# A two-pass path for the last five experts of a mixture-of-experts layer, behind one runtime branch

## The chip, the cores and the metric

The kernel runs on one core of a Trainium2 chip. The metric is the device time of one launch, in microseconds (us); beside it stands the span of one profiled execution, from its first to its last instruction. Engines are named as the profile names them: PE is TensorE's matmul, PEld its weight load, DVE is VectorE, ACT is ScalarE, POOL is GpSimd, SP is SyncE, which issues all the DMAs.

## The reference, cut to what matters

A two-layer decoder trunk on 256 tokens of width 2048, in float32. The second layer ends in a top-2-of-8 mixture of SwiGLU experts:

```python
def moe_swiglu(x, w_router, w_gu, w_down):       # x: 256 tokens x 2048
    logits = xt @ w_router                       # 256 x 8
    top_vals, top_idx = lax.top_k(logits, 2)
    gates = ...                                  # softmax over the two, 0 elsewhere
    for e in range(8):
        y = y + gates[:, e:e + 1] * swiglu(xt, w_gu[e], w_down[e])   # 2048 -> 2 x 1408 -> 2048
```

With the reference's own inputs (its default seed) the router gives the eight experts 42, 47, 57, 114, 53, 34, 109 and 56 tokens, as its formulas give when they are evaluated. These counts are data: the program learns them only when it runs.

## The kernel before

Every matmul of a weight runs in three passes, because float32 is kept as a pair of rounded parts. `load` (L98 to L110) issues one DMA from SP into a `raw` buffer (4 x 512 columns on 128 partitions, 1 MB; 768 KB where the block is 384 wide or only three chunks deep). ACT casts it to `wh` (L107), DVE subtracts to get the remainder `wl` (L108). The pools give five `raw` buffers and four of `wh` and of `wl`. `mm3` (L117 to L119) then multiplies, for each 128-row chunk of the weight, x-high by `wh`, x-high by `wl` and x-low by `wh`, with the 128 token slots as the stationary operand and up to 512 weight columns moving.

In `moe` every expert takes at most 128 tokens at once. `top2` picks experts, triangular matmuls turn the picks into positions, and `gather` builds for a pair of experts a 0/1 matrix `Dt` and multiplies it with the tokens (L837), so that PE itself collects the tokens of both experts, transposed, in 64 matmuls of 256 columns; ACT copies the results to `xe` (L839). `slots` inside it transposes `Dt` and picks the gate of each slot. The gather of the first pair runs inside `lead`, between the token casts and the first weight loads. The later pairs are gathered in four quarters during the down projection of the expert before them.

`expert_up` runs six accumulations of 16 chunks (gate and up, 512, 512 and 384 columns wide) and, for each width, `swiglu`: ACT applies silu (L527), DVE multiplies (L528), PE transposes (L181), ACT and DVE split the result (L174, L175). `expert_down` runs four accumulations of 11 chunks; ACT and DVE scale and split each (`yh` L896, `yl` L897), PE spreads it back over the two token tiles (L900, L901), DVE adds it to `h` (L234) and, for the last expert, takes the statistics (L236). One expert is 36 loads: 16 + 8 of `odd_moe_gu`, 8 + 4 of `odd_moe_down`, together 2048 x 2816 x 4 + 1408 x 2048 x 4 bytes = 34.6 MB.

The experts run in the order 0 to 7, written out, so that a scheduler at build time can weave the instructions of neighbouring stages together on each engine; each engine then runs its own list in order. Behind the last expert SP loads the gains and biases of the last LayerNorm (`gb`, L192), `final_norm` writes the output, and a branch (L729) stands ready for an expert with more than 128 tokens. Every engine takes that branch by itself: it loads the value into a register (L728) and compares. Here it is not needed and its body is jumped over.

## Time and profile before

| | |
|---|---|
| time, median of 3 runs (lowest to highest) | 2174.81 us (2173.45 to 2175.77) |
| the profiled execution: its own time | 2175.96 us |
| the profiled execution: span, first to last instruction | 2174.2 us |
| mean granted TensorE clock (1.0 is 2.4 GHz) | 0.994 |
| moved by DMA | 537.80 MB, mean 247 GB/s |

The profiled execution is one run and lies within 0.06% of the median. A busy PE in the profile is not PE at its peak: each matmul is shown until its modelled end, so neighbours overlap; how fast matmuls follow one another is read from their starts. DVE and ACT show an instruction's whole duration too, and the next may start some 0.08 us before the end shown.

### The profile page before, as it was taken

Reading aid. Unit: us, or ns where it says so; the run is one execution under the profiler, and the core shown is the slowest. Engines: PE = TensorE matmul, PEld = TensorE weight load, DVE = VectorE, ACT = ScalarE, POOL = GpSimd, SP = SyncE. Lnnn points to the kernel's source line nnn. Section 1 sums busy time; section 2 is a strip of 40 time slices with the busy share of each in tenths; the row PEclk is TensorE's granted clock in tenths of the full one; section 3 lists DMA queues with packets and bytes.
Section 4 is the critical chain, followed back from the end, with each engine's and each line's share of the span. In section 5 each row is a group of like instructions: output and inputs, shape, how many; then the busy total and the mean of one; then the engine's idle time right before and its main releaser. Section 6 shows DMA issues by size and latency. Waiting matters only on the chain.

```text
span 2174.2 us, 24450 instructions
## 1 busy us (share of the span) xinstructions
PE 2140.0 (98%) x9955; PEld 1781.5 (82%) x9956; DVE 1456.7 (67%) x1225; ACT 1146.6 (53%) x962; POOL 1.6 (0%) x6
## 2 busy tenths in 40 slices
PE   9999999999999999999999999999999999999996
PEld 7888888888888888888788887888888888888884
DVE  5443566554454644556676546898889888888988
ACT  5444355343333433343644335766766767676764
POOL 0000000000000000000000000000000000000000
PEclk9999999999999999999999999999999999999998
DMA  8544645555454554545544643899989999998995
GB/s 347 217 147 145 233 180 208 211 194 191 157 215 172 213 189 169 204 169 218 213 182 166 235 155 117 320 352 357 340 331 367 347 336 342 346 352 322 371 351 213
DMA packets 82198, 537.80 MB, mean 247 GB/s; under 512 B 9504, under 2 KB 10656, under 8 KB 28192
## 3 DMA queue, kind: packets, MB, share of 16 engines
q1 hardware_dynamic: 82080, 536.18, 66.3%
q8 instruction: 80, 1.31, 0.2%
q14 instruction: 38, 0.31, 0.0%
HBM read 534.04 MB, written 2.10 MB: 247 GB/s over the span
## 4 chain that ended last, share of the span: by engine, by line
PE 93%; DVE 3%; ACT 2%; DMA 1%; issue 0%; SPq 0%; DVEq 0%; ACTq 0%
PE acc L118 29%; PE acc L119 28%; PE acc L117 28%; PE ps L181 2%; DVE wl L108 1%; PE ps L837 1%; ACT wh L107 1%; PE ps L900 1%; DMA raw<-in_odd_moe_down_dram 1%; DMA raw<-in_even_w_in_dram 1%; PE ps L901 1%; ACT lnT L259 0%; PE ps L575 0%; PE acc L135 0%; PE acc L629 0%
## 5 line engine op out<-in xcount | busy, mean ns | idle before, releaser
L108 DVE TENSOR_TENSOR wl<-raw,wh 128x2048 fp32r<-128x2048 f32 (+2 forms) x519 | 1121.3, 2178 | 391.5 <-ACT wh L107 390.8
L107 ACT CAST wh<-raw 128x2048 fp32r<-128x2048 f32 (+2 forms) x519 | 935.4, 1824 | 442.1 <-PE acc L119 399.3
L118 PE MATMUL acc<-wl,xh 128*128 128x512 f32 x928 | 363.3, 392 | 1.1 <-DVE wl L108 1.1
L117 PE MATMUL acc<-wh,xh 128*128 128x512 f32 x928 | 361.8, 390 | 0.1
L119 PE MATMUL acc<-wh,xl 128*128 128x512 f32 x928 | 361.6, 390 | 0.0
L118 PE MATMUL acc<-wl,xe 128*128 128x512 f32 (+1 forms) x752 | 280.7, 373 | 0.1
L119 PE MATMUL acc<-wh,xe 128*128 128x512 f32 (+1 forms) x752 | 279.4, 372 | 0.0
L117 PE MATMUL acc<-wh,xe 128*128 128x512 f32 (+1 forms) x752 | 278.6, 371 | 0.5 <-ACT wh L107 0.5
L118 PE MATMUL acc<-wl,hTh 128*128 128x512 f32 x704 | 277.3, 394 | 1.1 <-DVE wl L108 1.0
L119 PE MATMUL acc<-wh,hTl 128*128 128x512 f32 x704 | 276.1, 392 | 0.0
L117 PE MATMUL acc<-wh,hTh 128*128 128x512 f32 x704 | 274.8, 391 | 0.0
L118 PEld LDWEIGHTS acc<-wl,xh 128*128 128x128 f32 x928 | 174.4, 188 | 37.0 <-DVE wl L108 1.5
L117 PEld LDWEIGHTS acc<-wh,xh 128*128 128x128 f32 x928 | 174.2, 188 | 37.1 <-ACT xh L174 0.5
L119 PEld LDWEIGHTS acc<-wh,xl 128*128 128x128 f32 x928 | 174.4, 188 | 35.7 <-DVE xl L175 0.2
L118 PEld LDWEIGHTS acc<-wl,xe 128*128 128x128 f32 x752 | 141.2, 188 | 21.2 <-DVE wl L108 1.8
L117 PEld LDWEIGHTS acc<-wh,xe 128*128 128x128 f32 x752 | 141.2, 188 | 20.7 <-ACT wh L107 0.8
L118 PEld LDWEIGHTS acc<-wl,hTh 128*128 128x128 f32 x704 | 132.3, 188 | 30.3 <-DVE wl L108 3.5
L119 PEld LDWEIGHTS acc<-wh,xe 128*128 128x128 f32 x752 | 141.3, 188 | 19.0
L117 PEld LDWEIGHTS acc<-wh,hTh 128*128 128x128 f32 x704 | 132.3, 188 | 28.3
L119 PEld LDWEIGHTS acc<-wh,hTl 128*128 128x128 f32 x704 | 132.4, 188 | 26.4
L174 ACT CAST hTh<-ps 128x512 fp32r<-128x512 f32 (+1 forms) x46 | 26.2, 569 | 180.4 <-PE ps L181 180.4
L117 PE MATMUL acc<-wh,x0h 128*128 128x512 f32 x256 | 104.1, 409 | 2.5 <-ACT wh L107 2.5
(201 smaller groups left out, 1820.0 us busy)
## 6 DMA issues: line engine op xcount, KB each, us to landing
raw<-in_odd_moe_gu_dram SPq DMA_DIRECT2D x128, 1024.0 KB, 6.9
raw<-in_even_ffn_gu_dram SPq DMA_DIRECT2D x88, 1024.0 KB, 4.8
raw<-in_odd_moe_down_dram SPq DMA_DIRECT2D x64, 1024.0 KB, 7.0
raw<-in_odd_moe_gu_dram SPq DMA_DIRECT2D x64, 768.0 KB, 6.1
raw<-in_even_ffn_down_dram SPq DMA_DIRECT2D x44, 1024.0 KB, 4.8
raw<-in_odd_w_in_dram SPq DMA_DIRECT2D x32, 1024.0 KB, 4.8
raw<-in_even_w_in_dram SPq DMA_DIRECT2D x30, 1024.0 KB, 5.0
raw<-in_odd_moe_down_dram SPq DMA_DIRECT2D x32, 768.0 KB, 6.8
```

What stands on the lines that cost most here:

```text
L107: nc.scalar.copy(wh, raw)
L108: self.wl_ins = nc.vector.tensor_tensor(wl, raw, wh.bitcast(F32), ALU.subtract)
L117: mm(acc, xh, wh, start=first, stop=False)
L118: mm(acc, xh, wl, start=False, stop=False)
L119: mm(acc, xl, wh, start=False, stop=last)
L174: self.nc.scalar.copy(hi, src)
L181: self.nc.tensor.transpose(ps[:, j * P:(j + 1) * P], src[:, j * P:(j + 1) * P], self.ident)
L837: mm(o, xtok[t, c // 8][part][:, cs], Dt[t].rearrange("p a b -> p (a b)"), start=j == 0 and t == 0, stop=t == 1, skip_group_check=True)
L900: nc.tensor.matmul(ps, DT[:, t, :], yh, start=True, stop=False)
L901: nc.tensor.matmul(ps, DT[:, t, :], yl, start=False, stop=True)
```

## The change

Expert 0 runs as before, but its tokens are gathered alone. While it runs, a new step `order` on DVE sorts experts 1 to 7: those with more than 64 tokens first, the rest behind, in their old order. It leaves the permuted expert numbers (`ids`), positions and gates, and the count of experts above 64 (`full`). SP loads `ids` into registers, and the weight DMAs of all later experts take their address from them. The first two of the sorted list run in the old three-pass path. Then all engines meet one `If`: if at most two experts are above 64, the other five run as `slim_expert`; if not, the `Else` runs the old path for them.

A slim expert has 64 slots. Its stationary operand holds x-high in columns 0 to 63 and x-low in columns 64 to 127, so a chunk needs two matmuls (with `wh` and with `wl`) and the rows 64 to 127 of the accumulator hold the low part's product. `fold` copies the accumulator by ACT and adds its lower rows to its upper ones with one more matmul; this is done for the six up accumulations. The down projection does the same with the split `hT`, and the spreading over the tokens, whose slot matrix names the 64 slots in both halves, sums the two. Nothing of the body is issued ahead of the branch (`EARLY = 0`), and the pools keep their sizes. The pieces of `expert_down` become the functions `down_loads` and `scatter`, the pieces of `gather` the function `slots`, with the same instructions.

```diff
+SLIM = 64
+EARLY = 0
+FATS = 2
+REST = NEXP - 1
...
-        nc.sync.dma_start(raw, src)
+        self.issued = nc.sync.dma_start(raw, src)
...
+        self.fold = pm.tile([P, P], F32R, tag="fold", name="fold", bufs=1)
+        nc.gpsimd.memset(self.fold[:, SLIM:].bitcast(F32), 0.0)
+        nc.gpsimd.tensor_copy(self.fold[:, :SLIM], self.ident[:, SLIM:])
...
-        gat = self.gather(xtok, [pos1[t][:, 0:2] for t in range(NT)], gg, 0, 0)
+        gat = self.gather(xtok, [pos1[t][:, 0:1] for t in range(NT)], gg, 0, 0, num=1)
...
+        def gate_cols(t, gates, at, num):
+            gv = gg[t][:, 1, at:at + 2 * num].rearrange("p (e s) -> p e s", s=2)
+            nc.scalar.copy(gv[:, :, 0], gates)
+            nc.vector.tensor_tensor(gv[:, :, 1], gates, gv[:, :, 0].bitcast(F32), ALU.subtract)
...
-        for e in range(NEXP):
-            cur = gat
-            hT = self.expert_up(e, cur, e % 2, None if e else first)
-            if e == 0:
+        many = pm.tile([P, REST], F32, tag="many", name="many", bufs=1)
+        nc.vector.tensor_scalar(many, cnt[:, 1:NEXP], float(SLIM), None, ALU.is_gt)
+        ids, posP, full = [], [], pm.tile([P, 1], I32, tag="full", name="full", bufs=1)
+
+        def gather(k, num):
+            return self.gather(xtok, [posP[t][:, k:k + num] for t in range(NT)], gg, NEXP + k, 0, num=num)
+
+        def gather_slim(k, num):
+            return self.gather_slim(xtok, [posP[t][:, k:k + num] for t in range(NT)], num)
+
+        def prepare():
+            order = self.order(many, pos1, gates, gate_cols, posP, full)
+            ins, v = nc.values_load_multi_w_load_instructions(
+                order[0:1, :], engines=[mybir.EngineType.SP], min_val=1, max_val=REST)
+            self.after(ins[0], self.issued)
+            ids.extend(v)
+
+        hT = self.expert_up(0, gat, 0, first, prepare)
+        gat[4]()
+        cur, gat = gat, gather(0, FATS)
+        gat[4]()
+        self.expert_down(0, cur, 0, hT, True, None, gat[3])
+        for p in range(FATS):
+            hT = self.expert_up(ids[p], gat, p)
+            self.expert_down(ids[p], gat, p, hT, False, None)
+        full_v = nc.values_load(full[0:1, 0:1], min_val=0, max_val=REST)
+        src = i["odd_moe_gu"][ids[FATS], 0]
+        early = [self.load(src[k]) for k in range(EARLY)]
+        with tc.If(full_v < FATS + 1) as slim:
+            at = 0
+            A, step = gather_slim(FATS, 2)
+            for q in range(4):
+                step(q)
+            for k in range(FATS, REST):
+                ahead = partial(gather_slim, k + 1, REST - k - 1) if k == FATS + 1 else None
+                nxt = self.slim_expert(ids[k], k - FATS - at, A, gg, NEXP + k, fstats if k == REST - 1 else None,
+                                       early if k == FATS else None, ahead)
+                if nxt is not None:
+                    A, at = nxt, 2
+        with slim.Else():
+            for k in range(FATS, REST, 2):
+                num = min(2, REST - k)
+                gat = gather(k, num)
                 gat[4]()
-            step = None
-            if e % 2 and e + 1 < NEXP:
-                gat = self.gather(xtok, [pos1[t][:, e + 1:e + 3] for t in range(NT)], gg, e + 1, 0)
-                gat[4]()
-                step = gat[3]
-            self.expert_down(e, cur, e % 2, hT, e == 0, fstats if e == NEXP - 1 else None, step)
+                for q in range(4):
+                    gat[3](q)
+                for p in range(num):
+                    hT = self.expert_up(ids[k + p], gat, p, early=None if k + p > FATS else early)
+                    self.expert_down(ids[k + p], gat, p, hT, False, fstats if k + p == REST - 1 else None)

         G, B = self.load_gb(i["odd_ln2_g"], i["odd_ln2_b"])
         self.final_norm(fstats, G, B)
...
+    def order(self, hv, pos1, gates, gate_cols, posP, full):
...
+        self.after(v.tensor_reduce(H, hv, AX.X, ALU.add), self.wl_ins)
+        v.tensor_copy(full, H)
+        v.tensor_tensor(sq, rows(hv), square(C_LOWER), ALU.mult)
+        v.tensor_reduce(rank, sq, AX.X, ALU.add)
+        v.scalar_tensor_tensor(a, e7, H, rank, ALU.add, ALU.subtract)
+        v.tensor_tensor(b, rank, a, ALU.subtract)
+        v.tensor_tensor(b, b, hv, ALU.mult)
+        v.tensor_tensor(a, a, b, ALU.add)
+        v.tensor_tensor(perm, rows(a), square(C_PLACE), ALU.is_equal)
+        v.tensor_scalar(b, e7, 1.0, None, ALU.add)
+        v.tensor_tensor(sq, perm, rows(b), ALU.mult)
+        v.tensor_reduce(b, sq, AX.X, ALU.add)
+        v.tensor_copy(ids, b)
+        for t in range(NT):
+            g = tile("gateP", [P, R], bufs=2)
+            x = tile("posP", [P, R], bufs=2)
+            for dst, src in ((x, pos1[t]), (g, gates[t])):
+                v.tensor_tensor(sq, perm, rows(src[:, 1:NEXP]), ALU.mult)
+                v.tensor_reduce(dst, sq, AX.X, ALU.add)
+            gate_cols(t, g, 2 * NEXP, R)
+            posP.append(x)
+        return ids
+
+    def gather_slim(self, xtok, pos, num):
...
+        slots = self.iota1[:, :SLIM].unsqueeze(1).to_broadcast([P, 2, SLIM])
+        d4 = []
+        for t in range(NT):
+            d = pm.tile([P, num, 2, SLIM], F32R, tag="Dt", name="d4", bufs=2)
+            for p in range(num):
+                nc.vector.tensor_scalar(d[:, p], slots, pos[t][:, p:p + 1], None, ALU.is_equal)
+            d4.append(d)
...
+        def quarter(q):
+            for c in range(4 * q, 4 * q + 4, per):
+                if c % hold == 0:
+                    units[0] = self.unit("xs", shape=[P, hold, num, 2, SLIM])
+                ps = self.ps()
+                for j in range(per):
+                    cs = slice((c + j) % 8 * P, ((c + j) % 8 + 1) * P)
+                    for part in range(2):
+                        o = ps[:, (2 * j + part) * w:(2 * j + part + 1) * w]
+                        for t in range(NT):
+                            mm(o, xtok[t, (c + j) // 8][part][:, cs], d4[t][:, :, 0, :],
+                               start=j == 0 and part == 0 and t == 0, stop=t == 1, skip_group_check=True)
+                for j in range(per):
+                    u = units[0][:, (c + j) % hold]
+                    nc.scalar.copy(u, ps[:, 2 * j * w:2 * (j + 1) * w].rearrange("p (a e s) -> p e a s", a=2, e=num))
+                    A[c + j] = u
+        return (A, d4), quarter
+
+    def slim_expert(self, e, p, gat, gg, col, stats, early, ahead):
...
+        def two(groups, lhs, w):
+            acc = self.acc()
+            n, k0 = sum(g[2] for g in groups), 0
+            for wh, wl, kc in groups:
+                for j in range(kc):
+                    mm(acc[:, :w], lhs(k0 + j), wh[:, j, :], start=k0 + j == 0, stop=False)
+                    mm(acc[:, :w], lhs(k0 + j), wl[:, j, :], start=False, stop=k0 + j == n - 1)
+                k0 += kc
+            return acc
+
+        def fold(acc, w):
+            c = self.pln.tile([P, CB], F32R, tag="lnT", name="low")
+            nc.scalar.copy(c[:, :w], acc[:, :w])
+            mm(acc[:, :w], self.fold, c[:, :w], start=False, stop=True, skip_group_check=True)
+
+        hT = []
+        for b, w in enumerate(EXP_W):
+            accs = [two(self.up_loads(e, b, u, early),
+                        lambda k: A[k][:, p], w) for u in range(2)]
+            for acc in accs:
+                fold(acc, w)
+            nch = w // P
+            s = self.pln.tile([P, CB], F32, tag="lnT", name="silu")
+            nc.scalar.activation(s[:, :w], accs[0][:, :w], AF.Silu)
+            nc.vector.tensor_tensor(s[:, :w], s[:, :w], accs[1][:, :w], ALU.mult)
+            pv = self.transpose4(s, nch)[:, :w].rearrange("p (c t) -> p c t", c=nch)[:, :, :SLIM]
+            h = pm.tile([P, 4, 2, SLIM], F32R, tag="hTh", name="hT2", bufs=3)
+            nc.scalar.copy(h[:, :nch, 0, :], pv)
+            nc.vector.tensor_tensor(h[:, :nch, 1, :], pv, h[:, :nch, 0, :].bitcast(F32), ALU.subtract)
+            hT.append(h)
+        DT, gs = self.slots([d4[t][:, p] for t in range(NT)], gg, col)
+        nxt, step = (None, None) if ahead is None else ahead()
+        for n in range(NCB):
+            if step is not None:
+                step(n)
+            acc = two(self.down_loads(e, n), lambda k: hT[k // 4][:, k % 4], CB)
+            self.scatter(acc, DT, gs, n, False, stats)
+        return nxt
...
+            if then is not None and b == 0:
+                then()
```

## Rows read from the trace of the kernel before

**Rows 1.** The page: busy us (share of the span) xinstructions of each engine.
```profile
PE 2140.0 (98%) x9955; PEld 1781.5 (82%) x9956; DVE 1456.7 (67%) x1225; ACT 1146.6 (53%) x962; POOL 1.6 (0%) x6
```

**Rows 2.** Windows, experts 2 and 5, then five: busy us (x), clock, DMA share, GB/s.
```profile
1538.94:1639.53 100.59, 100.59 (x484) 86.10 (x485) 86.16 (x59) 71.36 (x54) 0.00 (x0) 1.00 0.91 339
...
1840.60:1939.74 99.14, 99.12 (x480) 84.63 (x479) 85.17 (x57) 71.57 (x58) 0.00 (x0) 1.00 0.95 356
...
sum 501.40, PE 500.48 PEld 427.38 DVE 428.36 ACT 357.68 POOL 0.00; mean PE 100.10 PEld 85.47 DVE 85.67 ACT 71.54 POOL 0.00
```

**Rows 3.** Waits from 1538 to 2040 us: us in total, times, longest us.
```profile
ACT wh L107 <- PE acc L119: 28.7, 36, 1.3
...
PEld acc L118 <- DVE wl L108: 3.0, 6, 0.8
```

**Rows 4.** Timeline of PE, start us, us: matmuls of 512 columns.
```profile
1640.23 0.39 PE L118 MATMUL acc<-wl,hTh 128*128 128x512 f32 x1
1640.45 0.39 PE L119 MATMUL acc<-wh,hTl 128*128 128x512 f32 x1
```

**Rows 5.** Timeline of PE: matmuls of 384 columns.
```profile
1705.38 0.33 PE L117 MATMUL acc<-wh,xe 128*128 128x384 f32 x1
1705.55 0.33 PE L118 MATMUL acc<-wl,xe 128*128 128x384 f32 x1
```

**Rows 6.** Timeline of PE: eight gather matmuls of 256 columns.
```profile
1360.34 1.10 PE L837 MATMUL ps<-Dt,xtl 128*128 128x256 f32 x8
```

**Rows 7.** Groups of two experts, 1639.5 to 1840.5 us: busy us, mean ns, idle before.
```profile
L108 DVE TENSOR_TENSOR wl<-raw,wh 128x2048 fp32r<-128x2048 f32 x49 | 110.8, 2288 | 18.1 <-ACT wh L107 18.0
...
L839 ACT CAST xe<-ps 128x512 fp32r<-128x512 f32 x16 | 8.7, 592 | 3.8 <-PE ps L837 3.8
...
L175 DVE TENSOR_TENSOR hTl<-ps,hTh 128x512 fp32r<-128x512 f32 x4 | 2.8, 688 | 0.9 <-ACT hTh L174 0.8
```

**Rows 8.** Windows with the fastest DMA, columns as in rows 2.
```profile
17.50:47.50 30.00, 29.79 (x131) 24.36 (x131) 15.61 (x10) 15.26 (x13) 0.00 (x0) 1.00 1.02 416
...
2017.50:2047.50 30.00, 30.00 (x141) 25.47 (x141) 28.68 (x21) 21.75 (x15) 0.00 (x0) 1.00 0.99 398
2015.00:2065.00 50.00, 50.00 (x233) 42.40 (x232) 47.11 (x33) 36.97 (x25) 0.00 (x0) 1.00 0.99 377
```

**Rows 9.** The buffer raw, 1538.94 to 2040.34 us: time from issue to landing.
```profile
DMA to landing us min/median/max: 4.0/6.7/8.9
```

**Rows 10.** Timeline of ACT in expert 0, with idle time and what ended it.
```profile
1376.46 1.92 ACT L107 CAST wh<-raw 128x2048 fp32r<-128x2048 f32 x1 [0.80 <-PE acc L119]
```

**Rows 11.** Timeline of ACT at the end of expert 2.
```profile
1654.54 0.69 ACT L896 ACTIVATE yh<-acc,gs 128x512 fp32r<-128x512 f32 x1 [2.76 <-PE acc L119]
```

**Rows 12.** Groups of DVE in the router, 1336 to 1347 us.
```profile
L819 DVE TENSOR_SCALAR Dt<-c,pos 128x128 fp32r<-128x128 f32 x4 | 0.9, 284 | 0.0
...
L682 DVE SCALAR_TENSOR_TENSOR pos<-ps,sel 128x8 f32<-128x8 f32 x2 | 0.3, 162 | 0.0
```

**Rows 13.** The branch L729: duration ns min/median/max, first and last start.
```profile
L729 PEldq COMPARE_BRANCH  x1: 3370/3370/3370, 2155.0 to 2155.0; - x1
...
L729 DVEq COMPARE_BRANCH  x1: 72/72/72, 2169.0 to 2169.0; - x1
```

**Rows 14.** Timeline of the kernel's end.
```profile
2152.68 0.69 ACT L896 ACTIVATE yh<-acc,gs 128x512 fp32r<-128x512 f32 x1 [7.84 <-PE acc L119]
...
2157.49 0.74 DVE L224 SCALAR_TENSOR_TENSOR o<-h,mv,gb 128x512 f32<-128x512 f32 x1
```

**Rows 15.** Timeline of SP around the last weight load.
```profile
2134.99 0.33 SPq L106 DMA_DIRECT2D raw<-in_odd_moe_down_dram  x1
...
2136.31 1.23 SPq L192 DMA_DIRECT2D gb<-in_odd_ln_b_dram  x2
```

**Rows 16.** The buffer gb, 2130 to 2174 us: time from issue to landing.
```profile
DMA to landing us min/median/max: 6.2/7.4/8.3
```

**Rows 17.** Windows of the router, columns as in rows 2.
```profile
1340.00:1350.00 10.00, 6.88 (x41) 5.84 (x40) 8.46 (x40) 5.88 (x13) 0.00 (x0) 0.76 0.00 1
```

More of the change, by code (lines that the diff above doesn't have):

```diff
@@ L845, in slots @@
             for p in range(num):
[L846 to L854 removed]
+                DT, gs = self.slots([Dt[t][:, p, :] for t in range(NT)], gg, e + p)
                 DTs.append(DT)
@@ L857, in gather, with slots @@
         return xe, DTs, gss, quarter, slots
-    def expert_up(self, e, gat, p, first=None):
-        i, pm = self.i, self.pm
+    def slots(self, d, gg, col):
+        nc, pm = self.nc, self.pm
+        ps = self.ps()
+        for t in range(NT):
+            nc.tensor.matmul(ps[:, t * 256:(t + 1) * 256], d[t], gg[t], start=t == 0, stop=True,
+                             skip_group_check=True)
+        DT = pm.tile([P, NT, P], F32R, tag="DT", name="DT", bufs=3)
+        pv = ps.rearrange("p (a b) -> p a b", a=2)
+        nc.scalar.copy(DT, pv[:, :, 0:P])
+        gs = pm.tile([P, 1], F32, tag="gs", name="gs", bufs=4)
+        nc.vector.tensor_reduce(gs, pv[:, :, P + 2 * col:P + 2 * col + 2], AX.XY, ALU.add)
+        return DT, gs
@@ new lines, in order, with tile, rows, square @@
+    def order(self, hv, pos1, gates, gate_cols, posP, full):
+        nc, pm = self.nc, self.pm
+        v = nc.vector
+        R = REST
+        def tile(tag, shape, dt=F32, bufs=1):
+            return pm.tile(shape, dt, tag=tag, name=tag, bufs=bufs)
+        def rows(x):
+            return x.unsqueeze(1).to_broadcast([P, R, R])
+        def square(c):
+            return self.c[:, c:c + R * R].rearrange("p (a b) -> p a b", a=R)
+        e7 = self.c[:, C_IOTA7:C_IOTA7 + R]
+        rank, a, b = (tile(f"ord{k}", [P, R]) for k in range(3))
+        H = tile("ordH", [P, 1])
+        ids = tile("ids", [P, R], I32)
+        sq, perm = tile("ordsq", [P, R, R]), tile("perm", [P, R, R])
+        self.after(v.tensor_reduce(H, hv, AX.X, ALU.add), self.wl_ins)
[20 more added lines that the diff above has]
+        return ids
@@ L861, in expert_up @@
+    def expert_up(self, e, gat, p, first=None, then=None, early=None):
+        pm = self.pm
         xe = gat[0]
@@ L873, in expert_up @@
                     continue
-                groups = self.loads(i["odd_moe_gu"][e, b * 2 + u] if b < 2 else i["odd_moe_gu2"][e, u], w)
-                accs.append(self.block(groups, lhs, 0, w))
+                accs.append(self.block(self.up_loads(e, b, u, early), lhs, 0, w))
             hT.append(self.swiglu(pm, accs[0], accs[1], w, w // P, "m"))
+            if then is not None and b == 0:
+                then()
         return hT
@@ L887, in expert_down, with up_loads, down_loads, scatter @@
                 step(n)
-            groups = []
-            for k in range(0, EXP_KC, PIECE):
-                o, kc = k * CB * P, min(PIECE, EXP_KC - k)
-                src = i["odd_moe_down"][e, n][o:o + kc * CB * P].rearrange("(p m) -> p m", p=P)
-                groups.append(self.load(src))
-            acc = self.block(groups, lhs, 0)
-            yh = pm.tile([P, CB], F32R, tag="yh", name="yh", bufs=1)
-            yl = pm.tile([P, CB], F32R, tag="yl", name="yl", bufs=1)
-            nc.scalar.mul(yh, acc, gs)
-            nc.vector.scalar_tensor_tensor(yl, acc, gs, yh.bitcast(F32), ALU.mult, ALU.subtract)
-            for t in range(NT):
-                ps = self.ps()
-                nc.tensor.matmul(ps, DT[:, t, :], yh, start=True, stop=False)
-                nc.tensor.matmul(ps, DT[:, t, :], yl, start=False, stop=True)
-                self.add_stats(t, n, ps, None if stats is None else stats[t], first)
+            acc = self.block(self.down_loads(e, n), lhs, 0)
+            self.scatter(acc, DT, gs, n, first, stats)
+    def up_loads(self, e, b, u, early):
+        i = self.i
+        src = i["odd_moe_gu"][e, b * 2 + u] if b < 2 else i["odd_moe_gu2"][e, u]
+        if early is None or b or u:
+            return self.loads(src, EXP_W[b])
+        return early + [self.load(src[k]) for k in range(EARLY, src.shape[0])]
+    def down_loads(self, e, n):
+        groups = []
+        for k in range(0, EXP_KC, PIECE):
+            o, kc = k * CB * P, min(PIECE, EXP_KC - k)
+            src = self.i["odd_moe_down"][e, n][o:o + kc * CB * P].rearrange("(p m) -> p m", p=P)
+            groups.append(self.load(src))
+        return groups
+    def scatter(self, acc, DT, gs, n, first, stats):
+        nc, pm = self.nc, self.pm
+        yh = pm.tile([P, CB], F32R, tag="yh", name="yh", bufs=1)
+        yl = pm.tile([P, CB], F32R, tag="yl", name="yl", bufs=1)
+        nc.scalar.mul(yh, acc, gs)
+        nc.vector.scalar_tensor_tensor(yl, acc, gs, yh.bitcast(F32), ALU.mult, ALU.subtract)
+        for t in range(NT):
+            ps = self.ps()
+            nc.tensor.matmul(ps, DT[:, t, :], yh, start=True, stop=False)
+            nc.tensor.matmul(ps, DT[:, t, :], yl, start=False, stop=True)
+            self.add_stats(t, n, ps, None if stats is None else stats[t], first)
     def load_consts(self):
```

33 lines of the change are left out of this document (20 added, 13 removed).

## The prediction

> **What bounds the kernel now.** Three views, in this order. The page first: PE is busy 98% of the span [rows 1], but that says nothing of the stage that changes. So the windows next, one for each expert from its first load to the next one's [rows 2]: an expert lasts 100.3 us (501.40 / 5), of which PE is busy 100.10, DVE 85.67, ACT 71.54. The reader is to see that the runner-up is only 15% behind. Last the waits of the same stretch [rows 3]: ACT, whose casts start every weight's way, waits 36 times (28.7 us) for PE to give a buffer back, PE only 3.0 us for DVE. PE sets the pace here, and what a lighter PE is worth depends on what ends last behind it.
>
> **What the two passes take from PE.** Matmuls of 512 columns follow one another every 0.227 us (single steps of 0.22 to 0.23, [rows 4]), of 384 every 0.173 [rows 5], of 256 every (1.10 - 0.28) / 7 = 0.117 [rows 6]. An expert has 64 + 44 chunks of 512 columns and 32 of 384. Three passes are 3 x (108 x 0.227 + 32 x 0.173) = 90.2 us, two are 60.1. To these come six folds (1.3 us), the spreading (16 x 0.23 = 3.7), transposes and slots (1.4) and the gather. Gather matmuls of 128 and 192 columns have no row: half of 0.117 is the lower bound for 128, 0.117 the upper. The three rows lie on a line of 0.055 per 128 columns, so I take 0.06 and 0.09: 64 of each for five experts, 1.9 us for one. PE falls to 68.4 us for an expert. Were nothing else in the way, 5 x 31.7 = 158 us would go.
>
> **What is late next.** DVE. The stage keeps all 36 subtractions; it saves half the width of three `hTl` (0.69 us each whole, [rows 7]), some 0.9 us. Its floor is 85.67 - 0.9 = 84.7 us for an expert. DMA: 34.6 MB at the best rate that held for 30 us, 416 GB/s [rows 8], is 83.2 us. ACT: 71.54, less the pair gather's copies (8.7 for two experts, [rows 7]), plus 2.5 for the slim ones, plus six fold copies of some 0.59 (bounded by the `xe` copy, the same shape out of PSUM): 73 us. Two floors lie within 2 us of each other, fed through small buffers, on engines that run their lists in order, so the pitch p of a slim expert will be above 84.7. I take the share that DVE reached where it was busiest over 30 us, 28.68 / 30 = 0.956 [rows 8]: p = 84.7 / 0.956 = 88.6. The other end: 377 GB/s, the best 50 us [rows 8], gives 91.8; the best whole expert, 356 GB/s [rows 2], gives 97.2.
>
> The Trainium skill, page "DMA: Bandwidth & Descriptors", section Specifications, gives one core a limit of about 358 GB/s from HBM. By that figure p would be an estimated 96.6 and the time 2168.6. The 30 us at 416 GB/s disagree with it, and the measurement decides.
>
> The ring of five `raw` buffers must turn at that pace: 6.7 us from issue to landing at the median [rows 9], 1.92 for the cast [rows 10], 2.29 for the subtraction [rows 7], 10.9 in all, against 5 x 88.6 / 36 = 12.3. It fits with 1.4 us to spare, no more.
>
> **The terms around the stage**, counted from the start of `yh` of expert 2's last block, at 1654.54 [rows 11]; in the new kernel that is the end of the second fat expert.
> (a) The first gather is for one expert: 64 x (0.117 - 0.06) = 3.6 us less PE work in a stretch where PE is busy 9 tenths. Between 0 and -3.6; I take -3.
> (b) `order` is 24 small DVE instructions in one chain, 0.16 to 0.28 us each [rows 12], 4 to 7 us, and twice waits for an ACT copy that can stand behind a cast (2 x 1.92). Queued behind it are the subtractions of expert 0's second width, and PE waits for those. The cover: at 1376.46 ACT already waits for PE to free a `wh` [rows 10], so four loads of 2.8 us (100.3 / 36), 11 us of PE work, are ready. SP's register load of `ids` waits for the chain too, with the rest of expert 0's loads behind it; the same 11 us and the filled `raw` buffers cover it. Between 0 and 5; I take 1, the cover being the larger.
> (c) Entry. No instruction of the body may stand ahead of the branch. ACT's first cast comes behind `yh`: 0.69 + 1.92 us, so the first subtraction can't start before 2.6; DVE also has `yl`, two adds and four compares of 0.28 [rows 12] to do, and eight gather copies of 0.59 compete with the casts. SP runs ahead, passes the branch early and has the five buffers filled. The compare itself cost DVE 0.07 us [rows 13]. Between 2.6 and 8; I take 4. PE stands idle here, but it is not the bound behind it.
> (d) Five slim experts: 5 x 88.6 = 443, and 2 for the last one's statistics, which lay under PE before.
> (e) From the last subtraction to `yh`: three chunks by two passes, 1.6 us.
> (f) Leaving the body, each engine jumps over five unused experts. The one far jump that before shows, PE's, took 3.37 us; DVE's short one 0.07 [rows 13]. DVE's list of five experts holds more than 250 instructions, which is nearer to PE's case: 3.4 us on DVE, ahead of the last norm. Between 0 and 3.4.
> (g) From `yh` to the end as before: 2174.2 - 2152.68 = 21.5 us [rows 14]. The `gb` loads no longer run behind the last weight load [rows 15] but behind SP's jump: last issue + 0.4 + 3.4 + 2 + 8.3 (the longest landing, [rows 16]) = 14. They are needed at last issue + 6.7 + 1.5 + 1.8 + 1.6, then 4.8 (2157.49 - 2152.68) and 3.4 = 19.8. Hidden, with 6 us to spare; if SP must also see its last load land, 1 us late.
> The refactored pieces issue the same instructions and cost nothing; `fold`'s preparation is two POOL instructions, and POOL is idle. PE waits in each fold for ACT, with the next chunks queued behind: PE has 88.6 - 68.4 = 20 us to spare for an expert, and without that cover six folds of about 1 us would count.
>
> Sum: 1654.5 - 3 + 1 + 4 + 443 + 2 + 1.6 + 3.4 + 21.5 = 2128.0 against the span of 2174.2, a gain of 46.2 us. The profiled run took 2175.96, 1.15 above the median; on the median's scale the time is 2174.81 - 46.2 = 2128.6. In general it is 1685.6 + 5 p, and the gain is gone at p = 97.8.
>
> **Rivals.**
> 1. The ring or the DMA sets p. For it: 1.4 us of slack, and landings of up to 8.9 us [rows 9]. Against it: the 416 GB/s. p of 92 to 97, at 94.5 the time is 2158.
> 2. Slower: the ends of the blocks are laid bare. Behind the last subtraction of an up width come 1.8 us of matmuls, the fold copy 0.6, the fold 0.5, silu 0.6, transposes and `hT` 1.0, some 4.5 us that DVE doesn't fill if its list holds the multiply next; behind each down block 2.5 (matmuls and `yh`). 84.7 + 3 x 4.5 + 4 x 2.5 = 108, time 2226. It decides once more than 56% of these 23.5 us are uncovered (p above 97.8). For it: the fold is a new link, and `low` and `silu` share two buffers. Against it: in before the next casts are woven in between.
> 3. Slower: TensorE's clock. Before shows it at 0.76 of full where PE was busy 6.88 of 10 us in short pieces [rows 17]. At the lower level, 1.2 GHz, a slim expert takes 2 x 68.4 = 137 us, time 2370; it decides below a mean granted clock of 68.4 / 97.8 = 0.70. Against it: PE at half speed would have no idle time left, and busy stretches here stand at 1.00.
> The Trainium skill, page "TensorE: Matmul & The Clock Gate", section Part 1, describes this case: a thin matmul stage that waits for its weights falls back to the low clock again and again. By that rule this change would lose; the windows at 398 and 416 GB/s, where data was as fast as here, show 1.00 and disagree.
> 4. The change doesn't do what it says: the `Else` runs. With the counts of the reference's inputs (114 and 109, then 57, 56, 53, 47, 34 in some order) at most two are above 64, so it should not. Then the time is before's plus about 4 for the entry, 3.4 for the exit and 1 for the order: 2183.
> 5. Better: p of 84.7 to 86 and a cheap jump: 2103 to 2115.
>
> **How the numbers follow.** Forecast (p of 86 to 92, 2115 to 2146): 0.55. Rival 1, 0.17. Rival 5, 0.10. Rival 2, 0.10. Rival 3, 0.02. Rival 4, 0.03. No change at all, by a mixture of p near 97.8, 0.03. The lowest sum is p = 84.7 with -3.6, 0, 2.6 and no jump: 2109.1 - 0.6 - 1 - 1.4 - 3.4 = 2103. Upwards rival 1 counts to p = 96, 2166. From 2103 to 2166 holds 0.80; the forecast's own range is 2115 to 2146. Within 0.2% (4.3 us, about what a measurement of this kernel can tell from no change) lie p of 97 to 98.7: 0.05 with the edge of rival 1. Slower: 0.10 + 0.02 + 0.03 - 0.02 for what of them stays near = 0.13. Faster: 0.82.
>
> **What would show it.** In the body's windows: PE's matmul steps still 0.227 but with waits for `wl`; DVE busy some 95%, DMA near 390 GB/s, granted clock 1.00; 443 us between the body's first and last subtraction. DVE's wait at the exit near 3.4 us, and a DMA pause nowhere. I am wrong if DVE is below 90% there (rival 1 or 2: which of them tells who waits, ACT for DMA, or ACT and DVE for PE), if the clock is low, or if matmuls of L117 to L119 keep their number.

## The result, and the profile after

The time is 2186.16 us (median of 5 runs, 2185.47 to 2189.09) against 2174.88 (2173.45 to 2175.77): the ratio is 1.0055, with a 95% interval of 1.004 to 1.007. The change makes the kernel slower by 0.5%; 2128.6 was forecast, in a range of 2103 to 2166. The profiled execution has a span of 2184.4 us, 10.2 more than before.

The slim arm ran. The page shows PE with less to do [rows 1] and DVE the same:

```profile
PE 2055.4 (94%) x9286; PEld 1662.3 (76%) x9286; DVE 1456.7 (67%) x1249; ACT 1148.1 (53%) x994; POOL 1.9 (0%) x8
```

Windows of the second and third slim expert and of the whole body, from its first subtraction to its last (columns as in rows 2):

```profile
1751.65:1851.26 99.61, 81.30 (x336) 60.41 (x337) 84.63 (x61) 70.87 (x61) 0.00 (x0) 0.95 0.94 351
1851.26:1945.81 94.55, 81.55 (x360) 61.02 (x358) 85.03 (x57) 74.12 (x63) 0.00 (x0) 1.00 0.96 364
...
1664.40:2156.70 492.30, 402.41 (x1664) 297.41 (x1664) 424.56 (x284) 352.88 (x291) 0.00 (x0) 0.96 0.93 346
```

An expert takes 98.5 us (492.3 / 5), of which DVE is busy 84.9, and no engine is near 100% any more. DVE idles 13.5 us in each: it is busy 86% of the body, and the prediction's own sign of being wrong was less than 90%. Who makes it wait is told by the waits from 1640 to 2165 us, to be held against [rows 3]:

```profile
ACT low L1018 <- PE acc L1012: 69.6, 27, 4.3
...
DVE wl L119 <- ACT wh L118: 61.7, 47, 6.0
ACT yh L1098 <- PE acc L1012: 42.8, 16, 9.3
...
ACT wh L118 <- DMA raw<-in_odd_moe_gu_dram: 10.5, 14, 1.6
```

Landings are not what is missing (10.5 us). ACT waits 112 us for accumulators (9.3 of them behind the body), and DVE 62 us for casts (6.0 of them ahead of it). The two belong together, as ACT's and then DVE's timeline at the end of an up block show (a block is one accumulation):

```profile
1962.73 1.91 ACT L118 CAST wh<-raw 128x2048 fp32r<-128x2048 f32 x1 [0.64 <-DMA raw<-in_odd_moe_gu_dram]
1965.53 1.91 ACT L118 CAST wh<-raw 128x2048 fp32r<-128x2048 f32 x1 [0.89 <-DMA raw<-in_odd_moe_gu_dram]
1969.49 0.58 ACT L1018 CAST low<-acc 128x512 fp32r<-128x512 f32 x1 [2.05 <-PE acc L1012]
1969.98 5.50 ACT L118 CAST wh<-raw 128x2048 fp32r<-128x2048 f32 x3
```

```profile
1963.03 6.73 DVE L119 TENSOR_TENSOR wl<-raw,wh 128x2048 fp32r<-128x2048 f32 x3
1971.91 8.90 DVE L119 TENSOR_TENSOR wl<-raw,wh 128x2048 fp32r<-128x2048 f32 x4 [2.15 <-ACT wh L118]
```

The cast at 1962.73 is the block's last, the one at 1965.53 the next block's first. Behind that one stands `low` in ACT's list; it needs the old block's last matmuls (PE starts the last at 1969.07), and the other casts of the next block stand behind it. So DVE makes the two last subtractions of the old block and the one of the next for which it has a cast (until 1969.76), and then finds nothing to do until ACT has got `low` out of the way and made one more cast. This is how most ends of blocks stand in the new list: one or two casts of the next block ahead of `low` and of `yh`. The third expert has four, three and two ahead of its first three `low`, and from its first subtraction to the next expert's it takes 94.4 us, where the first, second and fourth take 97.9 to 99.8.

The entry is the second place. ACT, DVE, and a window of 10 us with its granted clock:

```profile
1654.25 0.69 ACT L1098 ACTIVATE yh<-acc,gs 128x512 fp32r<-128x512 f32 x1 [6.57 <-PE acc L130]
1660.22 0.65 ACT L995 CAST xs<-ps 128x256 fp32r<-128x256 f32 x2 [5.29 <-PE ps L991]
...
1662.46 1.91 ACT L118 CAST wh<-raw 128x2048 fp32r<-128x2048 f32 x1
```

```profile
1664.41 2.29 DVE L119 TENSOR_TENSOR wl<-raw,wh 128x2048 fp32r<-128x2048 f32 x1 [6.03 <-ACT wh L118]
```

```profile
1664.00:1674.00 10.00, 10.00 (x44) 9.61 (x44) 7.82 (x4) 9.15 (x16) 0.00 (x0) 0.50 0.56 198
```

From this `yh` to the first subtraction of the body are 10.2 us: ACT's first cast stands behind four copies of the gather (two pairs), and the gather runs at half the clock. The terms of the prediction's sum against this span:

| term | forecast | measured |
|---|---|---|
| up to `yh` of the second fat expert, (a) and (b) | 1652.5 | 1654.25 |
| (c) `yh` to first subtraction | 4 | 10.2 |
| (d) first to last subtraction | 445 | 492.2 |
| (e) last subtraction to `yh` | 1.6 | 3.3 |
| (f), (g) `yh` to the end | 24.9 | 24.5 |
| sum | 2128.0 | 2184.4 |

### The profile page after: what moved, and what is told of

It reads as the page before. It is cut to its first block, busy times and chain, and to the rows that moved or that the text cites. A ratio compares the mean times of both kernels' runs of the same rounds, so it can differ in the third digit from the quotient of the medians.

```text
span 2184.4 us, 23740 instructions
## 1 busy us (share of the span) xinstructions
PE 2055.4 (94%) x9286; PEld 1662.3 (76%) x9286; DVE 1456.7 (67%) x1249; ACT 1148.1 (53%) x994; POOL 1.9 (0%) x8
## 5 line engine op out<-in xcount | busy, mean ns | idle before, releaser
L1012 PE MATMUL acc<-wl,xs 128*128 128x512 f32 (+1 forms) x480 | 192.2, 402 | 42.9 <-DVE wl L119 41.9
L130 PE MATMUL acc<-wh,hTl 128*128 128x512 f32 x484 | 190.3, 393 | 0.0
L129 PE MATMUL acc<-wl,hTh 128*128 128x512 f32 x484 | 189.6, 392 | 0.0
L128 PE MATMUL acc<-wh,hTh 128*128 128x512 f32 x484 | 189.2, 391 | 0.0
L1011 PE MATMUL acc<-wh,xs 128*128 128x512 f32 (+1 forms) x480 | 185.0, 387 | 0.3 <-ACT wh L118 0.3
L1012 PEld LDWEIGHTS acc<-wl,xs 128*128 128x128 f32 x480 | 93.3, 194 | 82.6 <-DVE wl L119 69.7
L1012 PE MATMUL acc<-wl,hT 128*128 128x512 f32 x220 | 92.1, 419 | 26.7 <-DVE wl L119 26.6
L1011 PEld LDWEIGHTS acc<-wh,xs 128*128 128x128 f32 x480 | 93.5, 195 | 14.2 <-ACT wh L118 0.7
L129 PE MATMUL acc<-wl,x0h 128*128 128x512 f32 x256 | 100.6, 394 | 1.4 <-DVE wl L119 1.4
L130 PE MATMUL acc<-wh,xe 128*128 128x512 f32 (+1 forms) x272 | 101.1, 372 | 0.0
```

Of the source, the lines that this page charges most:

```text
L128: mm(acc, xh, wh, start=first, stop=False)
L129: mm(acc, xh, wl, start=False, stop=False)
L130: mm(acc, xl, wh, start=False, stop=last)
L1011: mm(acc[:, :w], lhs(k0 + j), wh[:, j, :], start=k0 + j == 0, stop=False)
L1012: mm(acc[:, :w], lhs(k0 + j), wl[:, j, :], start=False, stop=k0 + j == n - 1)
```

## The experiments

All are edits of the changed kernel. "Body" is the stretch from the first to the last subtraction of the five experts in the profiled execution; "entry" runs from `yh` of the second fat expert to the first subtraction (negative: it starts before that `yh`). The ratio is to runs of the kernel before, taken beside it. The profiled execution is one of a kernel's runs: in run 2 the longest of four (2148.47 to 2156.14 us), in run 14 the shortest (2144.85 to 2153.57), so bodies compare to some us only.

| run | time, us | ratio to before (95%) | entry | body |
|---|---|---|---|---|
| the change | 2186.16 | 1.0055 (1.004 to 1.007) | 10.2 | 492.2 |
| 1 one cast ahead | 2161.98 | 0.9945 (0.9932 to 0.9959) | 10.2 | 469.5 |
| 2 two casts ahead | 2152.75 | 0.9891 (0.9876 to 0.9906) | 9.7 | 463.4 |
| 3 frame alone | 2214.64 | 1.0184 (1.0171 to 1.0198) | 19.6 | 511.0 |
| 4 no branch | 2172.14 | 0.9989 (0.9978 to 0.9999) | -3.2 | 495.2 |
| 5 two ahead, no branch | 2149.87 | 0.9874 (0.9858 to 0.9891) | -3.2 | 470.7 |
| 6 four raw buffers | 2219.46 | 1.0191 (1.0178 to 1.0205) | 9.3 | 519.7 |
| 7 filler in the body | 2188.17 | 1.0062 (1.0048 to 1.0075) | 8.6 | 493.5 |
| 8 two ahead, three early loads | 2914.04 | 1.3399 (1.3381 to 1.3418) | -3.2 | 1231.5 |
| 9 two ahead, casts first | 2154.88 | 0.9900 (0.9885 to 0.9915) | 4.1 | 469.0 |
| 10 two ahead, six raw, three wl | 2157.99 | 0.9920 (0.9906 to 0.9933) | 9.8 | 440.1 |
| 11 9 and 10 together | 2158.78 | 0.9928 (0.9915 to 0.9942) | 4.1 | 447.2 |
| 12 two early loads | 2243.29 | 1.0311 (1.0297 to 1.0325) | -3.2 | 562.1 |
| 13 9 with PE kept busy at the entry | 2144.84 | 0.9859 (0.9842 to 0.9875) | 4.2 | 457.0 |
| 14 2 with PE kept busy at the entry | 2149.30 | 0.9889 (0.9872 to 0.9905) | 4.2 | 458.3 |

**1 and 2: the order of ACT's and DVE's lists.** In the body the loads of the next block are issued in the program before the end of the present one, and the order of some instructions is fixed (`AHEAD` is 1 or 2):

```diff
+            fold(accs[0], w, self.cast_ins)  # first low behind the width's last cast
+            cast, sub = self.peek(AHEAD)     # makes the next block's first loads
+            fold(accs[1], w, cast)           # second low behind that cast on ACT
...
+            self.after(nc.vector.tensor_tensor(s[:, :w], s[:, :w], accs[1][:, :w], ALU.mult), sub)
...
-        nc.scalar.mul(yh, acc, gs)
+        self.after(nc.scalar.mul(yh, acc, gs), cast)
```

> The slim body as in the change, but the cast of the next block's first load stands ahead of the block's last copy (low, yh) in ACT's list, and its subtraction ahead of the block's last product in DVE's list. Theory A (ACT works its list in order, waits 3.5 us at each block's end for the accumulator with the next cast behind, and DVE then waits for that cast): ACT's wait no longer holds back a subtraction; of DVE's 13 us of idle time in a slim expert 6 to 10 go, the pitch of a slim expert falls from 98 to 88 to 92, and the time from 2186 to 2136 to 2156. Theory B (the five raw buffers or the DMA set the pitch): the same bytes and buffers, so the pitch stays at 97 to 99 and the time at 2180 to 2192. Theory C (PE is the bound at its lower clock, 0.92 to 1.00 of full being granted in the slim windows): the time moves by less than 10 us, and PE waits for DVE less only where the clock falls further.

> As the kernel with one cast ahead, but two casts (and their subtractions) of the next block stand ahead of the block's last copy. Theory A: a block's end leaves DVE with 2 x 2.3 us of subtractions instead of one, which covers the whole chain of the last chunk's matmuls, low, fold and silu (4.5 us by the prediction); pitch 86 to 89, time 2125 to 2141, below the one with one cast. Theory B: no further change. Against both: low and yh come later by 1.9 us, and a PSUM buffer is free later; if that counts, it is no better than one ahead, 2136 to 2156.

Theory A holds in direction, and its size was too large: 24 us with one cast and 33 with two, at the same buffers and bytes, both short of their ranges. The names of the runs tell less than the edit does. One cast already stood ahead of every `low` in the changed kernel; what run 1 moves is the first `low` of each width, behind all four casts of the next block instead of mostly one or two, and DVE's multiply, behind the next block's first subtraction. Run 2 puts two casts ahead of the second `low` and of `yh`, where mostly one stood. ACT's and DVE's order were not changed one without the other. The waits from 1700 to 2090 us say which end of block each of the two mended. In run 1:

```profile
ACT wh L119 <- DMA raw<-in_odd_moe_gu_dram: 26.2, 29, 2.4
ACT yh L1129 <- PE acc L1043: 26.1, 12, 3.5
...
ACT low L1049 <- PE acc L1043: 10.0, 10, 1.8
```

In run 2:

```profile
DVE wl L120 <- ACT wh L119: 28.8, 34, 3.2
...
ACT yh L1129 <- PE acc L1043: 6.1, 9, 2.0
```

In the changed kernel the same stretch holds 54.7 us for `low`, 26.1 for `yh` and 42.7 of DVE's waits. In the down blocks one cast stood ahead of `yh` already, so the first edit leaves that wait as it was and the second removes it. What grows is ACT's wait for landings (10.5 to 26.2): the next limit. The pitch, a fifth of the body, stops at 92.7, not at the 86 to 89 expected of two casts.

**3: the frame alone.**

```diff
-        with tc.If(full_v < FATS + 1) as slim:
+        with tc.If(full_v < 1) as slim:
```

> The condition is made false for these inputs, so the five experts take the three-pass path of the kernel before behind the same branch, in the same order of experts. What remains of the change is its frame: the order of the experts, the entry, gathers that no longer lie in an expert's down blocks, and the exit. The prediction put these at 1 + 4 + 3.4 us: 2183. Theory A with the entry as the changed kernel shows it (10.2 us, of which some 3 lie at any expert's end, exit 4.3): 2184 to 2190, so that the slim stage itself gains next to nothing over three passes. A rival: gathers bare at the head of each pair cost PE's own time no more than before, but ACT and DVE wait: up to 2196.

Both were too low. This timeline of ACT at its entry shows why it is no measure of the slim stage's frame:

```profile
1662.33 0.74 ACT L916 CAST DT<-ps 128x256 fp32r<-128x256 f32 x2 [6.68 <-PE ps L912]
...
1666.11 6.64 ACT L895 CAST xe<-ps 128x512 fp32r<-128x512 f32 x13 [0.27 <-PE ps L893]
1672.50 3.83 ACT L118 CAST wh<-raw 128x2048 fp32r<-128x2048 f32 x2
```

A whole pair is gathered at the entry, 16 copies ahead of the first cast, and DVE starts 19.6 us after `yh`. What follows: behind a branch, with the gathers bare, two passes take 28.5 us less than three (2214.64 - 2186.16), 9.4 of them at the entry; the old order, three passes woven together without a branch, stays ahead of both.

**4 and 5: no branch.** The comparison and the second arm are left out (so the kernel serves only inputs with at most two such experts), alone and with two casts ahead.

> The slim body alone, with neither the comparison nor the other arm, so that it is woven with the end of the second fat expert and with the last norm. Theory: the frame's cost is entry 10.2 us against some 2.5 at any expert's end, and exit 4.3: 2186 - 8 - 4 = 2174, with the pitch in the four later slim experts unchanged at 97 to 99. Rival (the prediction's terms, entry 4 and exit 3.4): 2186 - 5 = 2181. If the pitch falls too, weaving over the ends of blocks is done by list order that the branch prevented, and then time falls below 2165.

> Two casts ahead and the slim body without comparison and second arm. Theory A with a separate price of the branch: the two gains add, 2153 - 14 = 2139 (2134 to 2144), with the pitch of the later slim experts at 91 to 93 as with two casts ahead. Rival: both take away the same idle time at the entry, so that the sum is less: 2143 to 2150.

Without the branch 14.0 us go, where 12 were expected. In spans: from `yh` to the last subtraction 492.0 in place of 502.4, from the last `yh` to the end 21.55 in place of 24.5. The pitches of the second to fourth expert are the same to 1 us (98.8, 94.4, 98.7 against 99.8, 94.4, 98.9): the branch is not what makes the pitch. In run 5 the rival holds: the branch is worth 2.9 us there, not 14, and not clear of the noise (0.9874 against 0.9891). That both edits fill the same idle time is argued, not shown.

**6: four raw buffers.**

```diff
-        self.praw = e(self.pool("raw", 5))
+        self.praw = e(self.pool("raw", 4))
```

> The changed kernel with four raw buffers in place of five (fewer loads in flight, nothing else). Theory A (list order, the ring of five has slack in the slim stage: 10.9 us of use per buffer against 13.6 at a pitch of 98): four buffers turn once in 4 x 2.72 = 10.9 us, just enough, so a slim expert stays within 98 to 102 and the stage loses at most 20 us. Theory B (the ring of five sets the pitch of 98): a buffer's turn takes 13.6 us, so with four the pitch is 36 x 13.6 / 4 = 122, and the slim stage alone loses 120 us. Stages ahead of it may lose time too; the windows of the slim experts decide.

The pitch is 103.9 (519.7 / 5), outside both expectations but by far nearer to A: 10.9 us for a buffer's turn was somewhat too little, 4 x 103.9 / 36 gives 11.5. A fifth buffer puts more loads under way, and each lands a little later (median 7.2 us against 6.8), so a turn takes 11.9 and five buffers allow some 36 x 11.9 / 5 = 86, an estimate: the ring did not set 98.

**7: PE filled in the body.** One useless matmul of 512 columns behind each load's matmuls.

```diff
                 k0 += kc
+                if k0 < n:
+                    self.keep_busy(1, self.c[:, :CB // 2].bitcast(BF16))
```

> The changed kernel with one matmul of 512 columns of no use behind every load's matmuls within a slim block (26 for an expert, 5.9 us of PE work where PE has some 15 us idle), so that PE pauses less. Theory C (the lower clock in stretches sets the later experts at 97 to 99.6 where the one at a granted clock of 1.00 takes 94.6): the clock rises to 0.98 to 1.00 and each of the later experts falls to 94 to 95, time 2186 - 3 x 3.3 = 2174 to 2180. Theory A alone: PE only gets more work, the wait of ACT at a block's end is the same or longer, the clock follows nothing of the time: 2184 to 2194.

Windows of its second and fourth slim expert:

```profile
1752.00:1849.90 97.90, 82.95 (x361) 59.86 (x362) 84.64 (x61) 71.01 (x61) 0.00 (x0) 0.98 0.95 350
...
1946.70:2044.10 97.40, 82.02 (x342) 56.51 (x342) 84.29 (x56) 68.65 (x54) 0.00 (x0) 1.00 0.96 356
```

The clock rises (0.95 to 0.98, 0.97 to 1.00), and these two experts take some 1.5 us less, but the third, at a clock of 1.00 in both kernels, takes 2.3 more: the five windows sum to 503.3 us against 503.2, and the time does not fall. Theory C is out for the pitch. The fill-in costs PE time too, so a small gain could be hidden in it.

**8 and 12: loads ahead of the branch.**

```diff
-EARLY = 0
+EARLY = 3        # in run 12: 2, without casts ahead
```

> Two casts ahead, and three loads of the first slim expert (with their casts and subtractions) placed ahead of the branch, so that ACT and DVE have finished weights when the body begins. Theory of the entry (10.2 us between yh and the first subtraction of the body, of which a branch of 3.8 us on PE and a gather with nothing beside it): three subtractions, 6.9 us of DVE work, are done before, so of the 10 us some 5 to 7 go: 2146 to 2148. Rival (the gather on PE and its copies on ACT set the entry, and weights are not late): no more than 2 us, 2151 to 2155. Dearer: wh buffers, four, are held by what is ahead, so that the last casts of the fat expert come later: 2155 to 2160.

Nothing of this was right. ACT's timeline in its body:

```profile
1951.11 1.90 ACT L119 CAST wh<-raw 128x2048 fp32r<-128x2048 f32 x1 [5.34 <-PE acc L1042]
...
1958.35 1.90 ACT L119 CAST wh<-raw 128x2048 fp32r<-128x2048 f32 x1 [4.86 <-PE acc L1042]
1965.59 1.90 ACT L119 CAST wh<-raw 128x2048 fp32r<-128x2048 f32 x1 [5.34 <-PE acc L1042]
```

One load every 7.24 us, each cast waiting for the matmuls of the load before it, as with a single `wh`. The 3.8 us on PE that the expectation puts at the branch lie at the stage's exit in the changed kernel (2161.45, 3772 ns); at the entry the comparison took PE 86 ns (1656.58). The new theory was tried with two early loads:

> The changed kernel with two loads of the first slim expert (with cast and subtraction) ahead of the branch, and no casts ahead at the blocks' ends. Theory for the 2914 us with three early loads: the wh and wl buffers of loads made ahead of the branch are read inside it and are not given back before its end, so that of four buffers one was left, and each load took a whole turn of cast, subtraction and matmuls, 7.24 us. With two early loads two are left: pitch at least 36 x 7.24 / 2 = 130, time 2186 + 5 x 32 = 2346 (2300 to 2400). Rival: the three early loads and the two casts ahead together made the four buffers wait for one another; then two early loads alone shorten the entry, 2178 to 2186.

The rival falls: the pitch is 112.4 (562.1 / 5), with ACT waiting 107.5 us in 390 for PE to free a `wh`. The theory has the right direction, its size was too large: a turn is 2 x 112.4 / 36 = 6.2 us, and the granted clock here is 0.99, where in run 8 it was 0.62. That buffers filled ahead of a branch and read inside it come back only behind it fits both runs; where the release is lost was not looked at.

**9, 13 and 14: the entry.** Run 9 puts two casts ahead of the gather's copies:

```diff
             A, step = gather_slim(FATS, 2)
+            self.entry = self.peek(2)[0]
...
+                    self.after(ins, self.entry)      # ins: the copy to xs
```

> Two casts ahead at every block's end, and at the entry of the body the first two casts of weights stand ahead of the gather's copies in ACT's list. Theory of the entry as it shows with two casts ahead: ACT waits 4.8 us for PE's first gather with the casts queued behind, and DVE waits 5.5 us for the first cast, whose data had landed. Then DVE's first subtraction starts when its four compares end, 5.5 us earlier, and the time is 2153 - 5.5 = 2147 (2145 to 2149). Rival: PE is the one that is late (its gather of 64 small matmuls ends some 10 us after the branch), the four wh buffers fill meanwhile and DVE waits there instead: 2150 to 2154.

The rival holds: DVE starts 5.6 us earlier and the time stays. DVE's timeline, and ACT's fifth cast:

```profile
1659.20 4.49 DVE L120 TENSOR_TENSOR wl<-raw,wh 128x2048 fp32r<-128x2048 f32 x2
1668.22 2.29 DVE L120 TENSOR_TENSOR wl<-raw,wh 128x2048 fp32r<-128x2048 f32 x1 [4.54 <-ACT wh L119]
...
1675.66 1.90 ACT L119 CAST wh<-raw 128x2048 fp32r<-128x2048 f32 x1 [1.59 <-PE acc L1045]
```

DVE's two subtractions are followed by 4.54 us of nothing: the third cast (1666.27) stands behind eight copies, for which ACT waits as the gather proceeds, and the fifth waits for PE to free a `wh`. PE is the late one.

Runs 13 and 14 give PE useless matmuls where it stood idle:

```diff
+        self.keep_busy(8, self.c[:, :CB // 2].bitcast(BF16))
         with tc.If(full_v < FATS + 1) as slim:
             at = 0
+            self.keep_busy(8, self.c[:, :CB // 2].bitcast(BF16))
```

> The kernel with casts first, and 8 matmuls of 512 columns of no use ahead of the branch and 8 behind it, where PE stood idle for 0.8 and 2.0 us and the granted clock then read 0.50 from 1658 to 1674. Theory of the clock at the entry: the body's first gather ran at 0.213 us a matmul (64 of them, 13.6 us) where the same step takes 0.112 at the full clock (7.2 us); with PE busy the clock stays at 1.00, the gather starts up to 2 us later but ends some 4 us earlier, and the time is 2155 - 4 = 2151 (2148 to 2152). Rival (the branch's own pause sets the entry, and the clock falls there whatever PE does): the fill-in only delays the gather, 2155 to 2159.

> Two casts ahead, the gather's copies ahead of the first casts as before, with the same 16 matmuls of no use around the branch. Theory of the clock at the entry: ACT gets the gather's results at full speed, so the first cast and the first subtraction come 1 to 3 us earlier and the gather's end 4 us earlier: 2149 to 2151. Rival: no change or a loss of the 2 us that the fill-in takes, 2152 to 2156.

In run 13 the clock theory holds, and by more than expected. Run 14 does not decide: its 2149.30 lies in the range of the theory, but its ratio to the kernel before is that of run 2 (0.9889 and 0.9891), though the clock stood at 1.00 there too. The window from 1664 to 1674 us of run 9, then of run 13:

```profile
1664.00:1674.00 10.00, 10.00 (x44) 9.71 (x45) 4.58 (x2) 7.31 (x14) 0.00 (x0) 0.50 0.66 256
```

```profile
1664.00:1674.00 10.00, 10.00 (x63) 8.93 (x63) 5.97 (x4) 9.75 (x15) 0.00 (x0) 1.00 0.84 324
```

The gather starts 1.5 us later (1660.5 against 1659.0) and the block's matmuls follow at 1667.8 instead of 1673.2 (all but two of them). The time falls from 2154.88 to 2144.84. Of the shorter body, 8.4 us lie in the first expert (99.4 to 91.0), where the entry is; some 5 lie in the last, and the entry does not explain those. Run 13 keeps both arms and beats the kernel before by 1.4%.

**10 and 11: six raw buffers**, with three of `wl` to make room.

```diff
-        wl = self.pw.tile([P, kc, w], F32R, tag="wl", name="wl")
+        wl = self.pw.tile([P, kc, w], F32R, tag="wl", name="wl", bufs=3)
...
-        self.praw = e(self.pool("raw", 5))
+        self.praw = e(self.pool("raw", 6))
```

> Two casts ahead, six raw buffers in place of five; wl has three buffers in place of four to make room. Theory (with the order of the lists mended, what keeps the pitch at 91 to 94 instead of the forecast 88.6 is the ring: ACT's casts wait 39 us for landings in 390 us, and a load is issued only when a subtraction has ended five loads back): landings come earlier, these waits go, pitch 88 to 90, time 2130 to 2142. Rival (the DMA's own rate: 372 to 381 GB/s at a share of 0.97 in these windows): pitch unchanged, landings take longer instead, 2148 to 2156. If three wl buffers are too few, PE sets the pace through them: above 2156.

> Both: two casts ahead, the first two casts of the body ahead of the gather's copies, six raw and three wl buffers. If the entry and the ring are separate prices: the sum of the two gains, 2153 - 5.5 - 15 = 2125 to 2138. If the wh buffers fill at the entry: as with six raw buffers alone.

The time missed, the pitch did not. Windows of the third and fourth slim expert of run 10, and the sum over all five:

```profile
1867.00:1955.00 88.00, 78.08 (x343) 59.37 (x342) 84.62 (x58) 72.15 (x58) 0.00 (x0) 1.00 0.99 395
1955.00:2041.50 86.50, 74.29 (x317) 55.30 (x316) 83.57 (x56) 69.75 (x53) 0.00 (x0) 1.00 1.00 399
...
sum 440.20, PE 386.81 PEld 292.74 DVE 418.74 ACT 354.22 POOL 0.00; mean PE 77.36 PEld 58.55 DVE 83.75 ACT 70.84 POOL 0.00
```

The pitch is 88.0, with 395 and 399 GB/s where run 2 had 374 and 383 in the same experts, and from 1790 to 2090 us ACT waits 13.6 us for landings, in run 2 30.9: with the order mended the ring does become the limit, as the theory said, and six buffers lift it. But `yh` of the second fat expert is now at 1678.9 instead of 1655.3: the stages ahead lose 23.6 us, all that the body gains (23.3). The expectation had named this case. The trace agrees with it: up to 1680 us DVE waits 343 us for PE to free a `wl`, for which it did not wait in run 2, and at expert 0's first `yh` the loss is already 23.1 us (1453.64 against 1430.52). No run has four `wl` with six `raw`. In run 11 the casts first bring nothing, as in run 9.

## Why the prediction was wrong

**The step that failed is (d)**, in the part "What is late next": p = 88.6, taken as DVE's floor over the share of 0.956 that DVE reached in the best 30 us of before [rows 8]. The floor was right (84.7 forecast, 84.9 measured). The body reached 0.862. The share was not to be had from that row: there PE was the late one, busy 30.00 of the 30 us, and DVE waited 2.8 us in all for casts. With PE light, the chain through a block's end is bare. That is rival 2, which had 0.10 because "in before the next casts are woven in between". They are in the new list too, but one or two of them do not cover it: ACT waits 2.05 us for the `low` shown above, and 3.81 us for the one at the next end of a block. Its mechanism was right only in part: DVE waits 9.5 us for the multiply that it names, and 61.7 for casts that ACT holds back. Its number came out by some luck. DVE's 13.5 us are 57% of its 23.5, where 56% makes a loss, but followed back to what ACT was waiting for only some 11 of them lie at the ends of blocks (38 us behind a `low`, 8 behind a `yh` and 9.5 for the multiply, in the five experts). Of the 9.9 us by which p was missed (0.4 of them are the last one's statistics, which the sum has apart), the order of the lists explains 5.8 (runs 1 and 2: 98.5 to 92.7), and the ring of five, on top of it, is worth 4.7 (run 10: 92.7 to 88.0). The prediction's ring, "fits with 1.4 us to spare", is rival 1: in the changed kernel it lay hidden behind rival 2, and it became the limit when that was gone. What six buffers give without the order was not tried.

The Trainium skill, page "PSUM — Partial Sum Buffer", section Engine vs sequencer instructions, calls the queues of ScalarE, VectorE and GpSimdE strict FIFO. The trace agrees: at the next end of a block a load that landed at 1978.12 was cast at 1982.40, behind a `low` for which ACT had waited 3.81 us.

**(c), the entry, was the second miss**: 10.2 for 4, and 13.3 more than before, where the first subtraction of that expert lies 3.1 us ahead of its `yh` (1651.42 against 1654.54). The prediction named the gather's copies as competitors but put the first cast right behind `yh`; ACT's list has copies first (5.29 us of waiting). And it charged the gather 0.06 us for a matmul of 128 columns: at full clock it is 0.112, the 0.117 of 256 columns [rows 6], and 0.213 at the entry's clock of 0.50. "PE stands idle here, but it is not the bound behind it" fell with runs 9 and 13: the low clock, 0.50 until 1674, followed the idle time, and PE was late behind it. Rival 3 had looked for the low clock in the stage as a whole; there the windows show dips to 0.95, and run 7 shows that they cost nothing measurable. At the entry it costs 8.4 us of the first expert (runs 9 and 13). The Trainium skill, page "TensorE: Matmul & The Clock Gate", section Part 1, says that a matmul stage which keeps pausing falls back to the low clock; the trace agrees with it in the direction, at the entry and in the dips.

**(a)** took 3 us for the first gather's narrower matmuls; by the same price of 0.112 it is 64 x 0.005 = 0.3, and 0.3 was measured for (a) and (b) together. **(b)** cost nothing that can be seen. **(e)** is 1.7 us longer. **(f) and (g)** were right: 24.5 for 24.9, and run 4, without the jump, has 21.55. The `gb` loads stay hidden. **The arm** was the slim one, as said.

## What to carry to other kernels

When a change takes the load off the engine that set the pace, look at the lists of the others at every point where an accumulation ends: an instruction that waits for the last result should stand behind enough feeding work for the next block. Here that was four casts for the first `low` and two for the other ends, in place of mostly one or two, and it was worth 33 us. A share that the runner-up reached while it was fed ahead is no forecast of what it reaches when it sets the pace. A branch can cost less by its jump (3 us here) than by what it forbids to weave across it (the rest of the 14.0 us of run 4; with the lists mended, in run 5, both together were worth 2.9). Loads ahead of it cost far more in the two runs in which their buffers were read inside.

## What was not expected of the hardware

A gather matmul of 128 columns steps at 0.112 us, one of 192 at 0.11 (1833.9 to 1835.3 in the changed kernel), one of 256 at 0.117: the width below 256 buys next to nothing. After pauses of PE of 0.8 and 1.6 us around the branch the granted clock read 0.50 through the gather, with PE busy 10.00 of 10 us; 16 matmuls placed in the pauses kept it at 1.00. The branch is not needed for it: in run 4, without one, PE paused 0.8 and 0.9 us in the same gather, and the clock fell as well:

```profile
1664.00:1668.00 4.00, 4.00 (x21) 4.00 (x20) 0.00 (x0) 1.30 (x4) 0.00 (x0) 0.50 0.84 295
```
